# Two heads' attention scores in the two row halves of the array, with packed queries

## The chip, the cores and the metric

One Trainium2 chip, one of its cores. The metric is the device time of one execution in microseconds (us), the median of several executions. TensorE (PE) multiplies matrices into PSUM, VectorE (DVE) and ScalarE (ACT) work on SBUF and PSUM, GpSimd (POOL) on SBUF, and SyncE (SP) issues most transfers.

## What is computed

A two-layer backbone over 512 latent tokens and 256 context tokens, width 1024. Layer 0 mixes tokens with a gated delta rule, layer 1 with windowed attention, and each layer ends with an expert retrieval (PEER). The change lies in the attention of layer 1, cut here to what matters:

```python
def window_attention(q, k, v, kc, vc, sinks):     # 16 query heads, 4 key heads, head width 64
    ...
    s_loc = jnp.einsum('bnqhgd,bnkhd->bnhgqk', qb, kw).astype(F32) * scale
    ...
    s_loc = jnp.where(valid[None, :, None, None], s_loc, NEG_INF)
    s_ctx = jnp.einsum('bnqhgd,bchd->bnhgqc', qb, kc).astype(F32) * scale
    ...
    p = jax.nn.softmax(jnp.concatenate([s_loc, s_ctx, sink], axis=-1), axis=-1)
    ...
    o = (jnp.einsum('bnhgqk,bnkhd->bnqhgd', p_loc, vw)
         + jnp.einsum('bnhgqc,bchd->bnqhgd', p_ctx, vc))
```

A score sums over 64 products, half of the 128 rows of the array.

## The kernel before

The program is recorded by a framework that places buffers, sets all waits and orders the instructions of each engine by a schedule of its own. The order in which the code writes instructions is an input to that schedule and not the result. A matmul in fp32 becomes two instructions, each with its own load of 128 columns of weights.

`swa` does the attention layer in two stages. The **projection stage** (lines 776 to 845) normalizes the tokens, multiplies by six column blocks of the input weights (`columns`, tiles `pj`), rotates the result `Q` for the positions, transposes it into PSUM (`ptq`, line 830) and copies it out. One 128-row piece of `ptq` holds two heads, the first in rows 0 to 63 and the second in rows 64 to 127. Line 836 (ACT) copies the first into `qT[0:64, i]` and line 837 (DVE) the second into `qT[64:128, i + 1]`. The other 64 rows of each of the 16 query tiles are zeros, set once on POOL (line 773), and `kT` holds two key heads one above the other in the same way.

The **score stage** (lines 853 to 910) goes over four blocks of 128 queries (`b`), two pairs of key heads (`kp`) and four groups `g`: 32 pairs of heads `s` = 0, 1, so 64 heads in all. For each head:

- PE multiplies its 128-row query tile (the weights) with the 256 context keys (line 866) and with the 2 or 3 key tiles of the window (line 867), into the tile `sc`, of which there are two. Since the other head's rows of the query are zero, all 128 rows can be summed.
- PE adds the masks by a bf16 matmul with the identity (lines 871, 874): one mask in blocks 0 and 3, two in blocks 1 and 2.
- DVE takes the maximum (line 878), `mx` and `nm` (lines 879, 882); ACT the exponential `pr` (line 885), after which `sc` is free; DVE divides (`den`, lines 889 to 891).
- PE transposes `pr` into `ptp` (line 894), of which there is one; ACT or DVE copies it into `pT` (lines 896, 898).

After four pairs PE multiplies with the values (`po`, line 902), each head in one half of the array's columns. After two such rounds the block goes through the output weights (`proj`, tiles `py`). In block 0 DVE and ACT also split these weights into two parts (`wh` line 294, `wl` line 295).

Of the kernel before, what the change touches and what calls it, by code (L numbers as in the profile page):

```python
# [8 lines left out]
F32 = mybir.dt.float32  # L9
# [11 lines left out]
SEQ = 512  # L21
CTX = 256
# [42 lines left out]
class Kern:  # L65
# [697 lines left out]
    def swa(self, xl, gate, xout, done, free):  # L763

        nc, A = self.nc, self.A
        TT = CTX + SEQ
        with ExitStack() as ctx:
            q = ctx.enter_context(self.pool("sq"))
            qT = q.tile([128, 16, SEQ], F32, name="qT")
            kT = q.tile([128, 2, TT], F32, name="kT")  # L770
            vN = q.tile([128, 6, KVH, HD], F32, name="vN")
            for i in range(16):
                nc.gpsimd.memset(qT[64 - 64 * (i % 2):128 - 64 * (i % 2), i, :], 0.0)
            with ExitStack() as c1:
                ph = c1.enter_context(self.pool("sh"))
                ps = c1.enter_context(self.pool("sps", space=PSUM))
                hi = ph.tile([128, KT, TT], F32R, name="hi")
                lo = ph.tile([128, KT, TT], F32R, name="lo")

                def norm(t0, t1, row):  # L780
                    with ExitStack() as c2:
                        pn = c2.enter_context(self.pool(f"sn{row}"))
                        xs = [pn.tile([128, D], F32, name=f"x{t}") for t in range(t0, t1)]
                        for t in range(t0, t1):
                            self.dma(xs[t - t0], xl[t])
                        s = slice(t0 * 128, t1 * 128)
                        self.norm_T(1, 0, xs, [(0, t1 - t0, row)], hi[:, :, s], lo[:, :, s], pn, ps, "tp", 3)

                norm(2, 6, 0)
                p = c1.enter_context(self.pool("sp"))  # L790
                rope = p.tile([128, 4, 2, 2, 16], F32, name="rope")
                self.dma(rope, A["rope"])

                def columns(n, tiles):
                    w = [self.wsplit(p, A["s_in"][n, i], "w", [4, 256], 2, 2) for i in range(2)]
                    Q = {}
                    for t in tiles:
                        s = slice(t * 128, (t + 1) * 128)
                        pj = ps.tile([128, 256], F32, name="pj", tag="pj", bufs=3)
                        for k in range(KT):  # L800
                            wh, wl = w[k // 4]
                            self.mm3(pj, hi[:, k, s], lo[:, k, s], wh[:, k % 4, :], wl[:, k % 4, :], k == 0, k == KT - 1)
                        self.tick(TICK["swa"], MIX["swa"])
                        if n == 5:
                            nc.scalar.copy(vN[:, t].rearrange("p h d -> p (h d)"), pj)
                            continue
                        qn = Q[t] = p.tile([128, 256], F32, name="Q", tag="Q", bufs=8)
                        nc.scalar.copy(qn, pj)
                        if t < 2:
                            continue  # L810
                        x = qn.rearrange("p (h a s c) -> p h a s c", h=4, a=2, s=2)
                        rt = p.tile([128, 4, 2, 2, 16], F32, name="rt", tag="rt", bufs=2)
                        for s_ in range(2):
                            for a in range(2):
                                nc.vector.tensor_tensor(
                                    rt[:, :, a, s_, :], x[:, :, a, 1 - s_, :],
                                    rope[:, t - 2, 1, a, None, :].to_broadcast([128, 4, 16]), op=OP.mult)
                        for a in range(2):
                            nc.vector.tensor_tensor(
                                x[:, :, a], x[:, :, a],  # L820
                                rope[:, t - 2, 0, a, None, None, :].to_broadcast([128, 4, 2, 16]), op=OP.mult)
                        for s_, op in ((0, OP.subtract), (1, OP.add)):
                            nc.vector.tensor_tensor(x[:, :, :, s_, :], x[:, :, :, s_, :], rt[:, :, :, s_, :], op=op)
                    if n == 5:
                        return
                    for m in range(2):
                        for ts in (tiles[0:2], tiles[2:]) if len(tiles) == 6 else (tiles,):
                            pt = ps.tile([128, 512], F32, name="ptq", tag="tp", bufs=3)[:, 0:len(ts) * 128]
                            for i, t in enumerate(ts):
                                nc.tensor.transpose(pt[:, i * 128:(i + 1) * 128], Q[t][:, m * 128:(m + 1) * 128],  # L830
                                                    self.ident)
                            if n == 4:
                                nc.scalar.copy(kT[:, m, ts[0] * 128:(ts[-1] + 1) * 128], pt)
                            else:
                                i = 4 * n + 2 * m
                                nc.scalar.copy(qT[0:64, i, :], pt[0:64])
                                nc.vector.tensor_copy(qT[64:128, i + 1, :], pt[64:128])

                for n in range(4):
                    columns(n, range(2, 6))  # L840
                done()
                norm(0, 2, 1)
                columns(4, range(6))
                columns(5, range(6))
            free()
            with ExitStack() as c1:
                p = c1.enter_context(self.pool("sa"))
                ps = c1.enter_context(self.pool("sas", space=PSUM))
# [3 lines left out]
                for b in range(4):  # L852
                    lo_t, hi_t = max(b - 1, 0), min(b + 1, 3)
                    nl = hi_t - lo_t + 1
                    NK = CTX + nl * 128
                    tiles = [0, 1] + [2 + t for t in range(lo_t, hi_t + 1)]
                    bs = slice(b * 128, (b + 1) * 128)
                    oh = p.tile([128, KT, 128], F32R, name="oh", tag="oh", bufs=2)
                    ol = p.tile([128, KT, 128], F32R, name="ol", tag="ol", bufs=2)
                    for kp in range(2):  # L860
                        pT = [p.tile([128, 5, 4, 128], F32, name="pT", tag="pT", bufs=3) for s in range(2)]
                        for g in range(4):
                            for s in range(2):
                                i = 8 * kp + 2 * g + s
                                sc = ps.tile([128, 1024], F32, name="sc", tag="sc", bufs=2)
                                nc.tensor.matmul(sc[:, 256:512], qT[:, i, bs], kT[:, kp, 0:CTX], start=True, stop=True)
                                nc.tensor.matmul(sc[:, 512:512 + nl * 128], qT[:, i, bs],
                                                 kT[:, kp, CTX + lo_t * 128:CTX + (hi_t + 1) * 128],
                                                 start=True, stop=False, skip_group_check=True)
                                if b > 0:  # L870
                                    nc.tensor.matmul(sc[:, 512:640], self.identb, self.neg_gt, start=False,
                                                     stop=b == 3, skip_group_check=True)
# [19 lines left out]
                                pt = ps.tile([128, 8, 128], F32, name="ptp", tag="ptp", bufs=1)  # L892
# [7 lines left out]
                        for j, t in enumerate(tiles):  # L900
                            for s in range(2):
                                nc.tensor.matmul(po[64 * s:64 * s + 64, :], vN[:, t, 2 * kp + s, :],
                                                 pT[s][:, j].rearrange("p g q -> p (g q)"), start=j == 0,
                                                 stop=j == len(tiles) - 1, tile_position=(0, 64 * s),
                                                 skip_group_check=True)
# [672 lines left out]
```

## Time and profile before

| | us |
|---|---|
| median of 3 runs | 4637.15 |
| lowest and highest run | 4635.31, 4638.45 |
| the profiled execution, its own time | 4645.18 |
| span of its trace, first to last instruction | 4643.4 |
| PE busy | 3892.9 (84%) |
| DVE busy | 3152.0 (68%) |
| ACT busy | 1787.6 (38%) |
| POOL busy | 1736.7 (37%) |

The profile is one execution with every instruction's start and duration. Its times are counted from the first instruction. The projection stage lies at about 2830 to 2966 us and the score stage at 2966 to 3184. A matmul's recorded duration contains its way through the array, so the step from one matmul's start to the next one's says how long it holds the engine.

### The profile page before, as it was taken

Reading aid. Unit: us, or ns where it says so; the run is one execution under the profiler, and the core shown is the slowest. Engines: PE = TensorE matmul, PEld = TensorE weight load, DVE = VectorE, ACT = ScalarE, POOL = GpSimd, SP = SyncE. Lnnn points to the kernel's source line nnn. Section 1 sums busy time; section 2 is a strip of 40 time slices with the busy share of each in tenths; the row PEclk is TensorE's granted clock in tenths of the full one; section 3 lists DMA queues with packets and bytes.
Section 4 is the critical chain, followed back from the end, with each engine's and each line's share of the span. In section 5 each row is a group of like instructions: output and inputs, shape, how many; then the busy total and the mean of one; then the engine's idle time right before and its main releaser. Section 6 shows DMA issues by size and latency. Waiting matters only on the chain. (4 is left out here: it accounts for less than half of the span.)

```text
span 4643.4 us, 65369 instructions
## 1 busy us (share of the span) xinstructions
PE 3892.9 (84%) x23123; PEld 3128.0 (67%) x23123; DVE 3152.0 (68%) x7853; ACT 1787.6 (38%) x3426; POOL 1736.7 (37%) x1461
## 2 busy tenths in 40 slices
PE   6979999647798869999999997897946778888896
PEld 4857778545577668877877776765845666666664
DVE  3663469976699878666843445664898996767544
ACT  4764554423234733322332223443336333333332
POOL 0000011754444462565633330000340756656542
PEclk9999999878899989999999998998978899999998
DMA  6725643868888997899988883201246999999998
GB/s 234 246 93 187 213 172 100 304 241 294 284 313 279 307 379 252 336 385 368 379 324 320 320 321 131 73 19 70 90 177 189 386 353 409 409 390 409 404 393 312
DMA packets 433624, 1261.21 MB, mean 272 GB/s; under 512 B 40720, under 2 KB 139920, under 8 KB 433296
## 3 DMA queue, kind: packets, MB, share of 16 engines
q0 software_dynamic: 195680, 711.02, 40.8%
q1 hardware_dynamic: 237616, 546.01, 33.0%
q8 instruction: 182, 2.98, 0.3%
q14 instruction: 146, 1.20, 0.1%
HBM read 1177.18 MB, written 79.69 MB: 271 GB/s over the span
## 5 line engine op out<-in xcount | busy, mean ns | idle before, releaser
L1171 POOL DMA_INDIRECT u<-p_u,idx x640 | 843.7, 1318 | 723.1 <-DVE u L1173 170.4
L295 DVE TENSOR_TENSOR wl<-w,wh 128x1024 fp32r<-128x1024 f32 x604 | 735.6, 1221 | 418.0 <-ACT wh L294 408.6
L1198 POOL DMA_INDIRECT v<-p_v,idxT x640 | 719.0, 1123 | 766.0 <-PE po L1205 441.8
L294 ACT CAST wh<-w 128x1024 fp32r<-128x1024 f32 x636 | 659.8, 1046 | 887.9 <-PE pu L84 223.7
L1173 DVE SCALAR_TENSOR_TENSOR u<-u,hg 128x1024 f32<-128x1024 f32 x640 | 767.9, 1218 | 211.3 <-DMA u<-p_u,idx 209.8
L83 PE MATMUL pu<-lo,wh 128*128 128x384 f32 (+1 forms) x2048 | 658.1, 321 | 82.6 <-ACT a L1269 54.3
L85 PE MATMUL pu<-hi,wl 128*128 128x384 f32 (+1 forms) x2048 | 656.8, 321 | 52.6 <-DVE wl L295 47.9
L84 PE MATMUL pu<-hi,wh 128*128 128x384 f32 (+1 forms) x2048 | 650.6, 318 | 0.0
L83 PE MATMUL pv<-wl,ah 128*128 128x512 f32 x1280 | 527.0, 412 | 100.2 <-DVE wl L295 94.1
L84 PE MATMUL pv<-wh,ah 128*128 128x512 f32 x1280 | 512.6, 400 | 0.0
L85 PE MATMUL pv<-wh,al 128*128 128x512 f32 x1280 | 508.8, 399 | 0.0
L83 PEld LDWEIGHTS pu<-lo,wh 128*128 128x128 f32 x2048 | 406.0, 198 | 128.0 <-ACT a L1269 69.6
L85 PEld LDWEIGHTS pu<-hi,wl 128*128 128x128 f32 x2048 | 406.5, 198 | 69.9 <-DVE wl L295 59.3
L84 PEld LDWEIGHTS pu<-hi,wh 128*128 128x128 f32 x2048 | 406.2, 198 | 6.0 <-issue 5.0
L83 PEld LDWEIGHTS pv<-wl,ah 128*128 128x128 f32 x1280 | 247.0, 193 | 232.6 <-DVE wl L295 126.4
L1205 PE MATMUL po<-v,W 128*32 128x512 f32 x2560 | 322.9, 619 | 41.8 <-DMA v<-p_v,idxT 41.8
L85 PEld LDWEIGHTS pv<-wh,al 128*128 128x128 f32 x1280 | 247.8, 194 | 60.3 <-issue 5.0
L95 ACT CAST ah<-a 128x384 fp32r<-128x384 f32 (+1 forms) x256 | 116.5, 460 | 439.3 <-PE pv L84 394.5
L1269 ACT ACTIVATE a<-pu 128x384 f32<-128x384 f32 (+1 forms) x256 | 111.3, 435 | 443.2 <-PE pu L85 434.6
L84 PEld LDWEIGHTS pv<-wh,ah 128*128 128x128 f32 x1280 | 248.1, 194 | 48.9 <-issue 0.8
L295 POOL TENSOR_TENSOR wl<-w,wh 128x1024 fp32r<-128x1024 f32 x32 | 78.9, 2473 | 516.9 <-ACT wh L294 467.5
L1250 PE MATMUL pg<-oa,ob 128*128 128x128 f32 x1280 | 174.7, 291 | 56.7 <-DVE oa L1241 34.6
(483 smaller groups left out, 7114.0 us busy)
## 6 DMA issues: line engine op xcount, KB each, us to landing
w<-p_ut SPq DMA_DIRECT2D x256, 512.0 KB, 6.7
w<-p_vt SPq DMA_DIRECT2D x256, 512.0 KB, 6.8
w<-adaw SPq DMA_DIRECT2D x96, 512.0 KB, 5.2
G<-st SPq DMA_DIRECT2D x20, 2048.0 KB, 12.5
w<-g_qkv SPq DMA_DIRECT2D x48, 512.0 KB, 4.7
Gt<-G SPq DMA_DIRECT2D x32, 768.0 KB, 7.9
w<-p_wq SPq DMA_DIRECT2D x32, 512.0 KB, 4.6
Gt<-G SPq DMA_DIRECT2D x32, 512.0 KB, 7.4
```

The costliest lines, as they stand in the source:

```text
L83: mm(out, lh, rl, start=start, stop=False)
L84: mm(out, lh, rh, start=False, stop=False)
L85: mm(out, ll, rh, start=False, stop=stop)
L95: self.nc.scalar.copy(hi, x)
L294: nc.scalar.copy(hi, w)
L295: (sub or nc.vector).tensor_sub(lo, w, hi)
L1171: nc.gpsimd.indirect_dma_start(out=u, out_offset=None, in_=A["p_u"], in_offset=bass.IndirectOffsetOnAxis(ap=idx[:, s:s + 1], axis=0))
L1173: pin(nc.vector.scalar_tensor_tensor(u, u, 1.0, h, op0=OP.mult, op1=OP.mult, accum_out=w[:, s:s + 1]))
L1198: nc.gpsimd.indirect_dma_start(out=v, out_offset=None, in_=A["p_v"], in_offset=bass.IndirectOffsetOnAxis(ap=idxT[:, t:t + 1], axis=0))
L1205: pin(nc.tensor.matmul(po[hf][32 * g:32 * g + 32, :], W[:, g, :], vs[g][:, hf * 512:(hf + 1) * 512], start=j == j0, stop=j == j1 - 1, tile ...
L1250: nc.tensor.matmul(pg[:, :, j], ob[:, j, :], oa[:, j, :], start=True, stop=True)
L1269: nc.scalar.activation(a.rearrange("p g t -> p (g t)"), pu, AF.Gelu)
```

## The change

`qT` has 8 tiles of 128 rows instead of 16, each with two heads and no zeros; the memsets are gone; one ACT copy takes both heads out of `ptq`. The score matmuls take 64 rows each: head 0 in array rows 0 to 63 and head 1 in rows 64 to 127 (`tile_position`), and the code writes the matmuls of both heads alternately before the masks.

```diff
-            qT = q.tile([128, 16, SEQ], F32, name="qT")
+            qT = q.tile([128, 8, SEQ], F32, name="qT")
...
-            for i in range(16):
-                nc.gpsimd.memset(qT[64 - 64 * (i % 2):128 - 64 * (i % 2), i, :], 0.0)
...
-                                i = 4 * n + 2 * m
-                                nc.scalar.copy(qT[0:64, i, :], pt[0:64])
-                                nc.vector.tensor_copy(qT[64:128, i + 1, :], pt[64:128])
+                                nc.scalar.copy(qT[:, 2 * n + m, :], pt)
...
+                            scs = [ps.tile([128, 1024], F32, name="sc", tag="sc", bufs=2) for s in range(2)]
+                            for c0, k0, k1, last in ((256, 0, CTX, True),
+                                                     (512, CTX + lo_t * 128, CTX + (hi_t + 1) * 128, False)):
+                                for s in range(2):
+                                    r = slice(64 * s, 64 * s + 64)
+                                    nc.tensor.matmul(scs[s][:, c0:c0 + k1 - k0], qT[r, 4 * kp + g, bs], kT[r, kp, k0:k1],
+                                                     start=True, stop=last, tile_position=(64 * s, 0),
+                                                     skip_group_check=not last)
                             for s in range(2):
                                 i = 8 * kp + 2 * g + s
-                                sc = ps.tile([128, 1024], F32, name="sc", tag="sc", bufs=2)
-                                nc.tensor.matmul(sc[:, 256:512], qT[:, i, bs], kT[:, kp, 0:CTX], start=True, stop=True)
-                                nc.tensor.matmul(sc[:, 512:512 + nl * 128], qT[:, i, bs],
-                                                 kT[:, kp, CTX + lo_t * 128:CTX + (hi_t + 1) * 128],
-                                                 start=True, stop=False, skip_group_check=True)
+                                sc = scs[s]
```

What the schedule makes of it on PE, at the start of the score stage (block 0, pairs 1 and 2), before and then after. A row is a matmul with its tiles and columns, or the load of the identity for a mask; numbers tell the `sc` tiles of the heads apart in the second fence.

```order
L866 MATMUL sc<-kT,qT 128x256
L867 MATMUL sc<-kT,qT 128x256
L874 LDWEIGHTS identb
L874 MATMUL sc<-neg_lt,identb 128x128
L866 MATMUL sc<-kT,qT 128x256
L867 MATMUL sc<-kT,qT 128x256
L874 LDWEIGHTS identb
L874 MATMUL sc<-neg_lt,identb 128x128
```

```order
L864 MATMUL sc_25672<-kT_24394,qT_24393 128x256
L864 MATMUL sc_25673<-kT_24394,qT_24393 128x256
L864 MATMUL sc_25672<-kT_24394,qT_24393 128x256
L864 MATMUL sc_25673<-kT_24394,qT_24393 128x256
L874 LDWEIGHTS identb_60
L874 MATMUL sc_25672<-neg_lt_64,identb_60 128x128
L874 LDWEIGHTS identb_60
L874 MATMUL sc_25673<-neg_lt_64,identb_60 128x128
L864 MATMUL sc_25718<-kT_24394,qT_24393 128x256 x2
L874 LDWEIGHTS identb_60
L874 MATMUL sc_25718<-neg_lt_64,identb_60 128x128
L864 MATMUL sc_25719<-kT_24394,qT_24393 128x256 x2
```

In pair 1 the two heads' matmuls stand alternately. From pair 2 on, both matmuls of head 0 stand together, then its mask, then both of head 1; so it is in all of the other 31 pairs, here the first of block 1 on PE after the change:

```order
L864 MATMUL sc_26231<-kT_24394,qT_24393 128x256
L864 MATMUL sc_26231<-kT_24394,qT_24393 128x384
L871 LDWEIGHTS identb_60
L871 MATMUL sc_26231<-neg_gt_62,identb_60 128x128
L874 LDWEIGHTS identb_60
L874 MATMUL sc_26231<-neg_lt_64,identb_60 128x128
L864 MATMUL sc_26232<-kT_24394,qT_24393 128x256
L864 MATMUL sc_26232<-kT_24394,qT_24393 128x384
L871 LDWEIGHTS identb_60
L871 MATMUL sc_26232<-neg_gt_62,identb_60 128x128
```

In blocks 1 to 3 the rows of PE, DVE and ACT stand as they did before, but for the line number of the scores. In block 0 DVE's order has moved, here after its first two maxima, before and then after the change:

```order
L889 TENSOR_TENSOR den<-sm 128x1
L878 TENSOR_REDUCE mx<-sc 128x1
L890 RECIPROCAL den<-den 128x1
L879 TENSOR_SCALAR mx<-mx,sink 128x1
L891 TENSOR_SCALAR pr<-pr,den 128x512
L878 TENSOR_REDUCE mx<-sc 128x1
L882 TENSOR_SCALAR nm<-mx 128x1
L295 TENSOR_TENSOR wl<-w,wh 128x1024
```

```order
L889 TENSOR_TENSOR den<-sm 128x1
L890 RECIPROCAL den<-den 128x1
L891 TENSOR_SCALAR pr<-pr,den 128x512
L295 TENSOR_TENSOR wl<-w,wh 128x1024
L878 TENSOR_REDUCE mx<-sc 128x1
L295 TENSOR_TENSOR wl<-w,wh 128x1024
L879 TENSOR_SCALAR mx<-mx,sink 128x1
L878 TENSOR_REDUCE mx<-sc 128x1
```

The first maximum of pair 2 now stands behind the division of pair 1 and one weight split, and a second split stands between the two maxima.

## Rows read from the trace of the kernel before

**Rows 1.** Windows: projection stage and blocks 0 to 3; busy us per engine, granted clock.

```profile
core 0: us, PE busy (x) PEld busy (x) DVE busy (x) ACT busy (x) POOL busy (x), PEclk, DMA share, GB/s
2872.00:2966.00 94.00, 91.19 (x730) 88.90 (x729) 49.57 (x187) 32.49 (x65) 0.00 (x0) 0.98 0.18 57
2966.00:3016.00 50.00, 34.40 (x154) 22.48 (x153) 36.33 (x106) 27.31 (x61) 0.00 (x0) 0.90 0.34 116
3016.00:3072.00 56.00, 52.20 (x306) 35.94 (x306) 38.89 (x114) 23.03 (x60) 0.00 (x0) 1.00 0.06 20
3072.00:3129.00 57.00, 53.12 (x313) 36.44 (x312) 39.23 (x114) 23.05 (x59) 0.00 (x0) 1.00 0.06 19
3129.00:3184.00 55.00, 46.90 (x285) 34.08 (x284) 38.32 (x121) 22.28 (x65) 0.00 (x0) 1.00 0.03 10
```

**Rows 2.** Timeline of PE, one pair in block 1 (start, us, instruction).

```profile
3067.11 0.70 PE L866 MATMUL sc<-kT,qT 128*128 128x256 f32 x2
...
3068.35 0.22 PE L874 MATMUL sc<-neg_lt,identb 128*128 128x128 bf16 x1
3068.40 0.65 PE L866 MATMUL sc<-kT,qT 128*128 128x256 f32 x2
...
3069.59 0.22 PE L874 MATMUL sc<-neg_lt,identb 128*128 128x128 bf16 x1
...
3072.22 0.70 PE L866 MATMUL sc<-kT,qT 128*128 128x256 f32 x2 [0.21 <-ACT pr L885]
```

**Rows 3.** Timeline of DVE and ACT in the same pair.

```profile
3069.85 0.82 DVE L878 TENSOR_REDUCE mx<-sc 128x1 f32<-128x640 f32 x1
...
3071.05 0.14 DVE L882 TENSOR_SCALAR nm<-mx 128x1 f32<-128x1 f32 x1
...
3071.29 0.79 ACT L885 ACTIVATE pr<-sc,nm 128x640 f32<-128x640 f32 x1 [0.19 <-DVE nm L882]
```

**Rows 4.** Views of the tiles qT and ptq and of line 773, whole program.

```profile
L866 PE MATMUL sc<-kT,qT x128: 377/382/764, 2966.1 to 3179.4; 128*128 128x256 f32 x128
L773 POOL MEMSET qT<- x16: 517/520/524, 2799.1 to 2807.7; 64x512 f32 x16
L836 ACT COPY qT<-ptq x8: 577/579/581, 2891.7 to 2931.8; 64x512 f32<-64x512 f32 x8
L837 DVE COPY qT<-ptq x8: 686/690/695, 2892.3 to 2932.6; 64x512 f32<-64x512 f32 x8
...
  PE pt L268: 0.4, 1
```

**Rows 5.** Timeline of PE where matmuls in column halves (L902) begin and end.

```profile
3020.65 1.07 PE L902 MATMUL po<-pT,vN 128*64 128x512 f32 x2
3021.66 0.38 PE L83 MATMUL py<-wl,oh 128*128 128x256 f32 x1
3021.88 0.28 PE L84 MATMUL py<-wh,oh 128*128 128x256 f32 x1
3022.00 0.28 PE L85 MATMUL py<-wh,ol 128*128 128x256 f32 x1
...
3024.32 0.22 PE L874 MATMUL sc<-neg_lt,identb 128*128 128x128 bf16 x1
3024.47 3.65 PE L902 MATMUL po<-pT,vN 128*64 128x512 f32 x14
```

**Rows 6.** Timeline of PE in layer 0, matmuls of 32 columns (L85) and 32 rows (L332).

```profile
262.35 0.40 PE L85 MATMUL pa<-lhi,awl 128*32 128x512 f32 x1
262.58 1.02 PE L537 MATMUL pe<-rr,cm 128*128 128x512 f32 x2
263.44 0.38 PE L538 MATMUL pe<-neg_lt,identb 128*128 128x512 bf16 x1
263.75 0.43 PE L332 MATMUL pa<-cm,abT 32*128 32x32 f32 x4
```

**Rows 7.** Timeline of PE and DVE, a pair of block 3.

```profile
3176.73 0.22 PE L871 MATMUL sc<-neg_gt,identb 128*128 128x128 bf16 x1
...
3177.26 0.68 DVE L878 TENSOR_REDUCE mx<-sc 128x1 f32<-128x512 f32 x1
```

## The prediction

> **What bounds the kernel now.** I read first the windows of the two stages that the change touches [rows 1]. In the projection stage PE is busy 91.2 of 94 us, so PE bounds it. In the score stage PE is idle 15.6 of 50 us in block 0, 3.8 of 56 in block 1, 3.9 of 57 in block 2 and 8.1 of 55 in block 3, while DVE, the next, is busy 36 to 39 us in each. So blocks 1 and 2 are close to PE's limit, while in blocks 0 and 3 waits between the engines count too. Then the timeline of one pair in block 1, to see which chain closes the circle. The scores of head 0 start at 3067.11 and the next pair's at 3072.22, a period of 5.11 us [rows 2]. Within it the scores and masks of both heads run without a pause until 3069.81 (the last mask's 3069.59 and its 0.22) [rows 2]; the maximum of head 1 follows at once, at 3069.85, and DVE's next rows up to `nm` at 3071.05 stand behind it in DVE's order; the exponential at 3071.29 waits for `nm` [rows 3]; when it is done, at 3072.08, `sc` is free and the next scores start 0.14 us later [rows 2, 3]. The score matmuls of both heads lie on this circle. What makes one of them longer makes the pair longer by as much.
>
> **The change, part by part.** The sum is made for the profiled execution (4645.18 us by its own time, span 4643.4), which took 8.0 us longer than the median of the runs, 4637.15; the 8.0 are taken off at the end.
>
> *Memsets.* 16 of 0.52 us on POOL, 8.3 us, go [rows 4]. They ran at 2799 to 2808, and the first reader of the query tiles starts at 2966.1 [rows 4]; that distance hides them. POOL has nothing else in either stage [rows 1]. Worth nothing; without that cover it would be 8.3 us.
>
> *Copies.* Eight DVE copies of 0.69 us go; the eight ACT copies of 0.58 us keep their 512 columns and take 128 rows instead of 64 [rows 4]. No row shows that rows cost time, and DVE has 44 us to spare in that stage [rows 1]. PE waited for the DVE copy once, 0.4 us [rows 4]. Between 0 and 0.4 us gained; I take 0.4.
>
> *The matmuls themselves.* Their number, their columns and the columns of weights stay. The gain would be that two heads run side by side. Matmuls in two column halves do that: 14 of them, each of 512 columns, take 3.65 us [rows 5]. An fp32 column takes about 0.85 ns here (from 3068.40 to 3069.59 stand 2 × 256 and 2 × 384 columns and one mask of 0.05 [rows 2], and two passes at 2.4 GHz are 0.83), so 512 take 0.43, and one after another the 14 would take 6.0 us. But that needs both heads' matmuls next to each other in PE's order, and the order shows this in pair 1 alone. In the other 31 pairs the masks of head 0, which take all 128 rows, stand between them: the `sc` tile of head 0 becomes free before that of head 1, and the schedule fills it at once. So of 32 pairs one gains, some 0.9 us of streaming, just before PE waits for the first exponentials anyway. I count nothing.
>
> *Going in and out of the halves.* Before, scores, masks and transposes all took the whole array. Whatever follows a mask starts 0.05 us after it, the time of its 128 bf16 columns (3068.35 to 3068.40) [rows 2]. Where the column halves begin, the step from the mask is 0.15 (3024.32 to 3024.47), 0.10 more [rows 5]. Where they end, two matmuls of 0.43 and the first load, 0.05, would bring 3020.65 to 3021.56; the next matmul starts at 3021.66, 0.10 more, and the one behind it 0.22 later instead of 0.12, since the first one's weights were not loaded ahead: another 0.10 [rows 5]. The only matmuls with fewer rows in this program, 32 rows in layer 0, start 0.31 after a matmul of 512 bf16 columns (0.21 at 2.4 GHz): again 0.10 more [rows 6]. So for each head I count 0.10 to enter, 0.10 for the first load of query weights, 0.10 to leave, and 0.03 to 0.10 for the first load of the mask's identity: 0.33 to 0.40, and I take 0.34. The lower end of the unknown is 0, since the row halves themselves are in no row of before, and one kind of narrow matmul pays nothing (second rival). The Trainium skill says in TensorEngine Tiling (Array Packing), Key Properties, that changing the tiling mode, not just the tile, drains TensorE. By that sentence each of the 31 pairs without neighbours drains four times; it gives no price, so the price stays that of the rows.
>
> *What of it lies on the path.* Blocks 1 and 2 have 16 pairs. Both heads are on the circle there, and PE has too little idle time to hide them: 32 × 0.34 = 10.9 us. In block 3, 8 pairs: the mask of a pair's second head ends at 3176.95 and its maximum starts at 3177.26 because DVE was busy [rows 7], so 0.31 of its 0.34 are covered; the first head has no such cover. 8 × 0.34 + 8 × 0.03 = 3.0; with no cover it would be 5.4. In block 0, 7 pairs pay; PE waits most there, and I let one head in two count: 7 × 0.34 = 2.4, between 0 and 4.8. DVE's new order there puts weight splits of 1.2 us before other maxima than it did; three of them more or fewer on the path are 3.6 us either way, and I take 0. Outside, the order of some 60 rows moves (a few transposes in the projections, some rows of layer 1's experts); nothing in them is added, and I give them 2 us either way.
>
> *Behind the stage.* The first weights of layer 1's routing now wait for ACT too, but stand on SP's queue behind loads of the attention's result, which come later. So what the score stage loses reaches the end.
>
> Sum: −0.4 + 10.9 + 3.0 + 2.4 = +15.9 us. 4645.2 + 15.9 = 4661.1 for a profiled execution, less 8.0 is **4653 us** for the median, 0.34% slower. About 0.2% (9.3 us) is what a measurement of this kernel can tell from no change, so the bounds are 4628 and 4646.
>
> **The rivals.**
>
> *Price paid, but hidden by waits.* PE's idle time in the stage is 15.6 + 3.8 + 3.9 + 8.1 = 31.4 us [rows 1], more than the whole price of 63 × 0.34 = 21.4. If DVE and ACT reach their limits first wherever they now nearly do, half of the sum stays: +8, 4645 us. Against it stand blocks 1 and 2, where the circle contains the matmuls.
>
> *No price.* The 32-column matmuls of layer 0 that use one place of the array alone are followed after 0.23 us for 512 columns [rows 6], as in any run of such matmuls. If a 64-row tile followed by a full mask is like this case, nothing changes but the 0.4: 4637 us. Against it stand the 32-row matmuls, whose start does show the 0.10.
>
> *The halves do run side by side: faster.* If PE's order, or PE itself past the order, let the two heads overlap in all pairs, a pair would stream one head's columns instead of two: 1.07 us less in blocks 1 and 2 (256 and 384 columns, four passes at 2.4 GHz) and 0.85 in the others, and would go in and out once. On the shares taken above that is −17 − 7 for the streams and +9 for the price of 32 excursions: −15, 4622 us. It decides wherever a mask no longer stands between two heads. For it speaks that column halves overlap in this very trace; against it the order, in which 31 of 32 pairs are split. The Trainium skill's page TensorEngine Tiling (Array Packing), Theoretical Speedup, gives up to 2 times for 64 rows; by it the score matmuls would take half, which is this rival and needs the neighbours as well.
>
> *A higher price.* If within a half the weights of the second key range are not loaded ahead either, each head pays two or three more loads of 0.10, and the lower pace lets the clock fall more often than the 0.90 that block 0 shows [rows 1]: +30, 4667 us.
>
> **How the numbers follow.** Chances: my forecast 0.50, hidden by waits 0.15, no price 0.20, side by side 0.05, higher price 0.10. The forecast's own range is 4646 to 4660, from 0.33 to 0.40 a head and the bounds of blocks 0 and 3. The range for 8 in 10 must take in no price and hidden by waits, and leaves out side by side and most of the higher price: 4634 to 4663. Slower by over 0.2%: nearly all of the forecast (0.49), the higher price and a third of the hidden case, 0.64. Within 0.2%: 0.31. Faster: 0.05.
>
> **What would show it.** After the change, in pairs of block 1: the step from the last score matmul to the first mask 0.1 longer than the columns, the loads of a score's first weights no longer ahead of the matmul, and the mask after them likewise; a period near 5.8 us instead of 5.11 where the exponential closes the circle; block 3 longer by 3 us, blocks 1 and 2 by 5 to 6 each. In pair 1 two score matmuls of different heads starting within 0.05 us of each other. The memsets' end and the copies should show as no shift of the first score matmul by more than 1 us. I am wrong if the masks follow the scores without a gap, or if DVE, not PE, ends the waits in blocks 1 and 2, or if the new order of block 0 alone moves its length by more than 4 us.

## The result, and the profile after

The changed kernel took 4671.7 us in the median of 4 runs (4654.5 to 4677.8), the kernel before 4637.8 beside it: a ratio of 1.0075, with a 95% interval of 1.0053 to 1.0096, so some 34 us slower. Beside the first experiments it was timed again: 4661.2 us in 6 runs, 1.0054 (1.0036 to 1.0073). Over these runs the mean is 4664.5 us for the changed kernel (10 runs) and 4636.9 for the kernel before (the 73 runs beside the experiments): 28 us more. The two measurements side by side give 34 and 22, so the 28 is itself known to some 6 us only. The forecast was 16 more, 4653 us, with a range up to 4663.

The profiled execution of the changed kernel took 4654.5 us, 10 less than the mean of its kernel, while that of the kernel before took 8 more than its own. So whole spans can't be compared, and the stage is read by itself. The windows of PE, cut at the first score matmul of each block and at the first transpose of layer 1's norm behind the last projection (us and length, busy time and instructions, granted clock, DMA share, GB/s), of the changed kernel:

```profile
core 0: us, PE busy (x), PEclk, DMA share, GB/s
2957.74:3011.04 53.30, 43.35 (x154) 0.71 0.32 109
3011.04:3074.19 63.15, 59.62 (x307) 0.92 0.05 18
3074.19:3134.22 60.03, 56.39 (x312) 1.00 0.05 18
3134.22:3227.42 93.20, 74.40 (x399) 0.87 0.10 36
```

and the last of these four windows in the kernel before; its first three are those of [rows 1] to within 0.3 us (50.19, 55.97 and 57.17 us, at 0.90, 1.00 and 1.00):

```profile
3129.39:3214.44 85.05, 65.52 (x399) 0.94 0.12 42
```

The reader is to see two things. Block 2 has the full clock in both and is 2.9 us longer. Blocks 0, 1 and 3 are 3.1, 7.2 and 8.2 us longer, and their clock is lower: 0.71, 0.92 and 0.87 instead of 0.90, 1.00 and 0.94. Twice the missing share times the length is the time at 1.2 GHz: 31 us of block 0 instead of 10, 10 us of block 1 instead of none, 24 instead of 10 in the last window. The four windows are 21.3 us longer together.

The last window needs care. In three further profiles of the changed kernel (table and samples below) it takes 89.2 to 89.8 us at 0.94, the clock of the kernel before, and most of the 10 us at 1.2 GHz that such a window shows lies at its end, where PE is idle for some 10 us ahead of the norm's transpose. The changed kernel, profiled again:

```profile
3141.76:3230.99 89.23, 69.64 (x399) 0.94 0.10 38
```

So the lower clock of the last window is the reading of one profile in four.

PE's timeline of the last pair of block 1, the one that answers to [rows 2] (start, us, instruction; in brackets the idle time before it and what ended it):

```profile
3068.72 1.34 PE L864 MATMUL sc<-kT,qT 64*128 64x256 f32 x4
3070.00 0.23 PE L871 MATMUL sc<-neg_gt,identb 128*128 128x128 bf16 x1
3070.06 0.22 PE L874 MATMUL sc<-neg_lt,identb 128*128 128x128 bf16 x1
3070.21 1.34 PE L864 MATMUL sc<-kT,qT 64*128 64x256 f32 x4
3071.49 0.23 PE L871 MATMUL sc<-neg_gt,identb 128*128 128x128 bf16 x1
3071.55 0.22 PE L874 MATMUL sc<-neg_lt,identb 128*128 128x128 bf16 x1
3071.61 0.72 PE L894 MATMUL ptp<-cm,pr 128*128 128x128 f32 x5
...
3074.19 0.48 PE L864 MATMUL sc<-kT,qT 64*128 64x256 f32 x1 [0.21 <-ACT pr L885]
```

From the second mask of head 0 to the scores of head 1 it is now 0.15 us, in [rows 2] 0.05: entering costs 0.10, as forecast. From the first score to the transposes it is 2.89 us, in [rows 2] 2.53 (3067.11 to 0.05 behind 3069.59), and the period grows from 5.11 to 5.47 us. So a pair pays 0.36, not the 0.68 of the forecast, and eight pairs of such a block 2.9.

Pair 1, the only one in which the two heads' matmuls alternate, in the same timeline:

```profile
2957.74 1.66 PE L864 MATMUL sc<-kT,qT 64*128 64x256 f32 x8
2959.34 0.29 PE L874 MATMUL sc<-neg_lt,identb 128*128 128x128 bf16 x2
```

Its eight matmuls of 256 columns take 1.60 us to the mask, hardly less than the 1.7 that eight of 256 columns at 0.85 ns would take one after another, though going in and out is in the 1.60 too. By the single starts, two matmuls of the one head begin 7 ns after one of the other (2958.276 and 2958.283, 2958.596 and 2958.603); the other four run one after another.

Where the clock is lost PE is not idle. Two windows of the changed kernel in block 0:

```profile
2970.00:2980.00 10.00, 9.37 (x26) 0.50 0.53 177
2980.00:2990.00 10.00, 8.55 (x25) 0.50 0.31 107
```

PE is busy 9.37 and 8.55 of 10 us and stays at 1.2 GHz, where the kernel before has 0.90 over the block with a busy share of 0.69 [rows 1]. In both kernels the clock first falls at the end of the wait of over 4 us behind pair 1; in the kernel before it then has 0.62 to 0.80 from 2970.06 to 2982.06, in steps of 4 us, and 1.00 from 2986.06 to 2998.06, in the changed kernel 0.50 all the way from 2965.74 to 2993.74.

### The profile page after: what moved, and what is told of

The parts are those of the page before. It is cut to its first block, busy times and chain, and to the rows that moved or that the text cites. A ratio compares the mean times of both kernels' runs of the same rounds, so it can differ in the third digit from the quotient of the medians.

```text
span 4652.7 us, 65323 instructions
## 1 busy us (share of the span) xinstructions
PE 3916.3 (84%) x23123; PEld 3124.8 (67%) x23123; DVE 3152.0 (68%) x7845; ACT 1789.0 (38%) x3426; POOL 1740.0 (37%) x1445
## 5 line engine op out<-in xcount | busy, mean ns | idle before, releaser
L1198 POOL DMA_INDIRECT v<-p_v,idxT x640 | 728.4, 1138 | 752.7 <-PE po L1205 427.1
L85 PE MATMUL pu<-hi,wl 128*128 128x384 f32 (+1 forms) x2048 | 653.4, 319 | 48.9 <-DVE wl L295 43.7
L85 PE MATMUL pv<-wh,al 128*128 128x512 f32 x1280 | 508.9, 399 | 0.0
L85 PEld LDWEIGHTS pu<-hi,wl 128*128 128x128 f32 x2048 | 402.6, 197 | 67.0 <-DVE wl L295 55.6
L85 PEld LDWEIGHTS pv<-wh,al 128*128 128x128 f32 x1280 | 246.3, 192 | 59.1 <-issue 4.2
```

Source lines behind the costliest of these rows:

```text
L85: mm(out, ll, rh, start=False, stop=stop)
L1198: nc.gpsimd.indirect_dma_start(out=v, out_offset=None, in_=A["p_v"], in_offset=bass.IndirectOffsetOnAxis(ap=idxT[:, t:t + 1], axis=0))
```

## The experiments

Three theories. A: only the going in and out of the halves costs. B: the halves also let TensorE's clock fall. C: the new order of block 0 on DVE and ACT costs the rest. Median and ratio of each kernel (beside runs of the kernel before on the same chip; the interval is 95%), and from its profile the length of the four windows in us, with the granted clock:

| kernel | us | ratio | block 0 | block 1 | block 2 | block 3 and projection |
|---|---|---|---|---|---|---|
| before | 4632 to 4639 | 1 | 50.2 (0.90) | 56.0 (1.00) | 57.2 (1.00) | 85.1 (0.94) |
| changed, again | 4661.2 | 1.0054 (1.0036 to 1.0073) | 53.2 (0.68) | 63.1 (0.92) | 60.0 (1.00) | 89.2 (0.94) |
| e1_halves | 4679.1 | 1.0092 (1.0078 to 1.0107) | 55.5 (0.69) | 63.2 (0.92) | 60.0 (1.00) | 96.8 (0.82) |
| e2_order | 4639.1 | 0.9996 (0.9986 to 1.0006) | 51.1 (0.87) | 56.0 (1.00) | 57.2 (1.00) | 86.1 (0.93) |
| e3_switch | 4652.0 | 1.0023 (1.0012 to 1.0034) | 50.6 (0.83) | 59.4 (1.00) | 60.3 (1.00) | 87.3 (0.95) |
| e4_mid | 4644.1 | 1.0026 (1.0014 to 1.0038) | 50.4 (0.90) | 58.8 (1.00) | 60.0 (1.00) | 85.0 (0.95) |
| e5_ends | 4656.4 | 1.0053 (1.0036 to 1.0070) | 55.6 (0.69) | 56.1 (1.00) | 57.2 (1.00) | 96.5 (0.82) |
| e6_adjacent | 4881.5 | 1.0532 (1.0507 to 1.0556) | 121.7 (0.66) | 124.5 (0.63) | 122.9 (0.67) | 121.4 (0.64) |
| e7_pinfull | 4912.5 | 1.0596 (1.0573 to 1.0618) | 128.6 (0.68) | 131.4 (0.70) | 133.1 (0.69) | 126.9 (0.70) |
| e8_onetile | 4703.8 | 1.0162 (1.0141 to 1.0184) | 70.2 (0.68) | 75.7 (0.82) | 76.3 (0.81) | 99.9 (0.81) |
| e9_onefull | 4739.1 | 1.0221 (1.0201 to 1.0241) | 75.1 (0.72) | 83.7 (0.83) | 85.4 (0.82) | 105.2 (0.84) |
| e10_fill | 4663.8 | 1.0068 (1.0055 to 1.0082) | 56.4 (0.70) | 59.7 (1.00) | 60.0 (1.00) | 92.3 (0.97) |
| e11_fullfill | 4645.8 | 1.0024 (1.0012 to 1.0035) | 49.9 (0.93) | 57.0 (1.00) | 57.2 (1.00) | 89.0 (0.96) |
| e12_fill16 | 4673.7 | 1.0072 (1.0049 to 1.0095) | 53.4 (0.90) | 72.9 (0.88) | 60.0 (1.00) | 99.7 (0.97) |
| e13_fullfill16 | 4657.4 | 1.0041 (1.0026 to 1.0056) | 50.8 (0.93) | 61.7 (1.00) | 57.2 (1.00) | 96.2 (0.96) |

**The parts of the change, each alone.** e1_halves takes the kernel before and gives only the two score matmuls 64 rows:

```diff
-nc.tensor.matmul(sc[:, 256:512], qT[:, i, bs], kT[:, kp, 0:CTX], start=True, stop=True)
+r, tp = slice(64 * s, 64 * s + 64), (64 * s, 0)
+nc.tensor.matmul(sc[:, 256:512], qT[r, i, bs], kT[r, kp, 0:CTX], start=True, stop=True, tile_position=tp)
...
```

> The row halves alone: the kernel before with its memsets, its 16 query tiles, its copies and its order of code, only the two score matmuls of a head read 64 rows at (0,0) or (64,0). PE's order in the score stage stays that of the kernel before but for a few transposes of block 0. Theory A (going in and out of the halves is all that costs): +14 to +17 us over the kernel before, granted clock in block 0 as before, about 0.90. Theory B (half of the rows lets TensorE's clock fall as well): +28 to +40 us, and block 0's granted clock near 0.67 as in the changed kernel. Theory C (the changed order of block 0 on DVE and ACT costs the rest): as A here, since that order is not taken over.

e2_order writes the score matmuls of both heads alternately, as the change does, and leaves them on 128 rows:

```diff
+scs = [ps.tile([128, 1024], F32, name="sc", tag="sc", bufs=2) for s in range(2)]
...
+for s in range(2):
+    nc.tensor.matmul(scs[s][:, c0:c0 + k1 - k0], qT[:, 8 * kp + 2 * g + s, bs],
+                     kT[:, kp, k0:k1], start=True, stop=last, skip_group_check=not last)
```

> The order of code alone: score matmuls of both heads written alternately as in the changed kernel, but over all 128 rows with the zeros, memsets and copies of the kernel before. Theories A and B: within 4 us of the kernel before. Theory C: +10 us or more.

e3_switch puts a 64-row matmul of two columns ahead of each head's full-array scores:

```diff
+nc.tensor.matmul(sc[:, 0:2], qT[r, i, bs], kT[r, kp, 0:2], start=True, stop=True, tile_position=(64 * s, 0))
 nc.tensor.matmul(sc[:, 256:512], qT[:, i, bs], kT[:, kp, 0:CTX], start=True, stop=True)
```

> The going in and out alone, with the array full while columns stream: the kernel before with one more matmul of 2 columns on 64 rows ahead of each head's scores (it writes columns of the score tile that nobody reads). It pays 0.3 us a head for going in and out, and some 0.1 to 0.3 for its own load and passes: 64 heads, of which about 50 count, +15 to +30 us, the same under all theories in time. What tells them apart is the clock: Theory A and C: what e1_halves loses is lost here too. Theory B: block 0's granted clock stays near 0.90, since the score matmuls use all rows, while in e1_halves it falls.

The changed kernel itself ran beside them:

> The changed kernel again, beside the three others on one chip: +30 to +36 us over the kernel before under all theories. Theory B: a profile that took longer than the one shown (span 4652.7) has more half clock in the score stage, above all in block 0 and the last block; theories A and C: the same clock and the difference elsewhere.

The changed kernel lost 22 us here in the medians, not the 30 to 36 expected. The halves alone cost more than the whole change, 40 us in the medians, and the code's order costs nothing. That speaks against C but does not rule it out: the schedule orders the rows of DVE and ACT in block 0 anew in e1_halves and in e2_order too, in each in a way of its own, so neither has the changed kernel's order. What rules it out for the clock are the pairs of equal order below. In block 0 the changed kernel is 2.3 us shorter than e1_halves (53.2 and 55.5). e3_switch goes in and out for every head as well, for one more matmul of two columns, but its scores stream over all rows: blocks 1 and 2 grow by 3.4 and 3.1, block 0 by 0.4, and the total by some 11 us, less than the 15 to 30 expected. What e1_halves loses beyond that goes with its clock: 0.69, 0.92 and 0.82 against 0.83, 1.00 and 0.95. But 0.83 is also below the 0.90 that theory B expected here (0.89 to 0.93 in three profiles of the kernel before), so going in and out may lower the clock of block 0 by itself; its one profile, in an order of its own on every engine, doesn't settle that.

**Where it is lost.** e4_mid and e5_ends are e1_halves with the condition `b in (1, 2)` or `b in (0, 3)` on the rows; e4_mid has the order of the kernel before on every engine, e5_ends that of e1_halves.

> Row halves in blocks 1 and 2 alone (32 of the 64 heads), everything else, the order on every engine too, as in the kernel before. Going in and out on the path costs 2.8 us a block at full clock (block 2 of the changed kernel and of e1_halves: 60.0 us against 57.2). Theory B (the clock falls where 64-row matmuls meet a stage in which PE has waits): blocks 0 and 3 keep the clock of the kernel before, block 1 starts from a raised clock and keeps it, so +5 to +8 us. Theory A (only the going in and out costs, each excursion alike): half of what e1_halves lost, +20 us.

> Row halves in blocks 0 and 3 alone, the order on every engine as in e1_halves. Theory B: +25 to +35 us, nearly all that e1_halves lost, with some 34 us of half clock in block 0 again and the clock still low when block 1 begins. Theory A: +20 us, and less if PE's waits in these blocks hide it.

Blocks 0 and 1 of e1_halves, block 1 of e4_mid and block 1 of e5_ends:

```profile
2965.44:3020.97 55.53, 44.77 (x153) 0.69 0.31 105
3020.97:3084.12 63.15, 59.61 (x306) 0.92 0.05 17
...
3010.73:3069.56 58.83, 55.31 (x306) 1.00 0.06 19
...
3030.33:3086.47 56.14, 52.16 (x307) 1.00 0.05 20
```

In the middle blocks alone the halves cost 2.9 us a block at full clock and nothing elsewhere. Block 1, which has 7.2 us more in the changed kernel, has 2.9 here: its other 4.3 us come with its low clock. That clock isn't left over from block 0. In the changed kernel, where block 1 begins at 3011.04, it is back at 1.00 some 14 us earlier and falls anew (all engines, then the granted clock):

```profile
2997.00:3007.00 10.00, 9.12 (x46) 4.86 (x45) 6.11 (x20) 5.34 (x15) 0.00 (x0) 1.00 0.00 0
3007.00:3017.00 10.00, 8.51 (x32) 4.44 (x30) 6.91 (x24) 2.63 (x9) 0.00 (x0) 0.74 0.00 0
3017.00:3027.00 10.00, 9.53 (x37) 5.02 (x38) 3.82 (x13) 3.42 (x10) 0.00 (x0) 0.75 0.01 2
```

It is at 1.00 up to 3011.04 and at 0.50 from 3013.04. With halves in block 0 alone (e5_ends) block 1 keeps 1.00, though a low clock at its start was expected, and so it does with halves in block 1 alone (e4_mid): this fall needs halves on both sides of the border. In the first and last block alone they cost 5.4 and 11.5 us at a clock of 0.69 and 0.82. Theory A, with the same price for each excursion, does not give this. The totals fit B less well than the windows do: e4_mid lost 12 us in the medians, more than the 5 to 8 of B (A said 20), of which its windows show 5.8; e5_ends lost 25, the low end of 25 to 35, of which its windows show 17.

**Is it the clock?** e10_fill adds to e1_halves, and e11_fullfill to the kernel before, eight matmuls a head whose result nobody reads, in blocks 0 and 3; e12_fill16 and e13_fullfill16 add sixteen. In each of the two sets the order on every engine is the same, so that its kernels differ by the row halves alone.

```diff
+for j in range(8 if b in (0, 3) else 0):
+    nc.tensor.matmul(pt[:, 7, :], self.identb, self.neg_gt, start=True, stop=True)
 for j in range(NK // 128):
     nc.tensor.transpose(pt[:, j, :], pr[:, j * 128:(j + 1) * 128], self.ident)
```

> The kernel e1_halves (row halves, order of code of the kernel before) with work that does nothing: in blocks 0 and 3 eight more full-array matmuls of 128 bf16 columns ahead of each head's transposes, into columns of their tile that nobody reads. At full clock they are 0.43 us a head, half of what the score streams lost in busy rows there. Theory B1 (half-busy rows let the clock fall): block 0's half clock comes down from 34 us to 20 or less, and block 0 is no longer than in e1_halves (55.5) although PE has 7 us more to do. Theory A or C (not the clock): half clock stays near 34 us and block 0 gets longer by up to 7 us.

> The control of e10_fill: the same filling matmuls in the kernel before, with the same order on every engine as e10_fill, so that these two differ by the row halves alone. Theory B1: e10_fill less this one is smaller than e1_halves less the kernel before (40 us): +10 to +25. Theory A or C: the same 40 us. If the 10 us of half clock that the kernel before has in block 0 are gone here, this one may be up to 5 us faster than the kernel before, else up to 14 us slower.

> e10_fill with sixteen filling matmuls a head in blocks 0 and 3 instead of eight. If the clock alone is what is left in block 0: the half clock there falls from 34 us to 15 or less, and block 0 gets shorter than e10_fill's 56.4 us although PE has 7 us more work at full clock; it is then 2 to 4 us longer than in e13_fullfill16. If something else holds block 0 back, its half clock stays near 34 us and it gets longer than 60 us, or the clock comes back and the block does not get shorter.

> The control: sixteen filling matmuls a head in the kernel before, with the same order on every engine as e12_fill16. Block 0 49 to 55 us with less than 10 us of half clock; e12_fill16 less this one is +10 to +14 us for the whole program if only going in and out is left (2.8 us a block), more if the clock still falls in one of them.

Windows of PE, block 0 and ten us of it, of e10_fill

```profile
2963.84:3020.27 56.43, 51.04 (x254) 0.70 0.31 103
...
2970.00:2980.00 10.00, 10.00 (x40) 0.50 0.46 166
```

and of e11_fullfill

```profile
2960.00:3009.85 49.85, 37.68 (x255) 0.93 0.34 117
...
2970.00:2980.00 10.00, 6.38 (x50) 1.00 0.43 135
```

With the halves PE is busy without a pause and stays at 1.2 GHz; with all rows it is busy 6.38 of 10 us and has 2.4 GHz. In blocks 1 and 3 the filling was enough: the clock is that of the control, and what is left is 2.7 and 3.3 us (59.7 and 57.0, 92.3 and 89.0). In the medians e10_fill is 18 us longer than e11_fullfill, within the 10 to 25 that theory B1 gave, where e1_halves had lost 40. In block 0 eight were not enough: it has 34 us at 1.2 GHz, as e1_halves has, against B1's forecast of 20 or less, and is 6.6 us longer than its control. Sixteen were. Block 0 of e12_fill16

```profile
2959.15:3012.58 53.43, 46.04 (x337) 0.90 0.31 109
```

and of e13_fullfill16

```profile
2965.24:3016.07 50.83, 41.40 (x338) 0.93 0.34 115
```

With twice the filling block 0 is shorter than in e10_fill, by 3.0 us, and 2.6 us longer than its control: the price of going in and out, and no more. In block 3 that price is 3.5 (99.7 and 96.2, at 0.97 and 0.96). Elsewhere e12_fill16 missed: block 1 is 11.2 us longer than in the control and fell to 0.88, and the totals are 16 us apart instead of the 10 to 14 expected, so the two kernels together are no proof of a total.

**Would the halves pay if they were neighbours?** e6_adjacent fixes the order of the scores and masks of a pair in the changed kernel (`self.pin(...)` around each of these matmuls keeps them in the order of the code), e7_pinfull is the same with full-array matmuls. e8_onetile gives a pair one score tile of four banks, so that both heads become free at once, and writes both heads' masks behind the four score matmuls; e9_onefull is its control with all rows and zeros.

```diff
-scs = [ps.tile([128, 1024], F32, name="sc", tag="sc", bufs=2) for s in range(2)]
+sc2 = ps.tile([128, 2, 1024], F32, name="sc", tag="sc", bufs=1)
+scs = [sc2[:, s] for s in range(2)]
```

> The changed kernel with the scores and masks of a pair kept in the order of the code, so that in all 32 pairs the matmuls of both halves are neighbours in PE's order and run side by side. It saves 0.85 to 1.07 us of streaming in each pair and goes in and out once instead of twice (0.17 a head on the path): 16 pairs of blocks 1 and 2 give 16 x (1.07 - 0.35) = 11.5 us back against the kernel before, less what head 0 loses by waiting for both score tiles. Theory B1 (the chip counts the rows that are busy): with both halves busy the clock in blocks 0 and 3 is as in the kernel before, total -20 to 0 us. Theory B2 (the chip counts the time that PE is busy, or the halves as such): the halves make PE idle longer and the clock falls as in the changed kernel or more, total +10 to +30 us.

> The control of e6_adjacent: the same fixed order of scores and masks with full-array matmuls and zeros. What it loses against the kernel before is the price of the fixed order (head 0 waits for both score tiles): 0 to +15 us under all theories; e6_adjacent minus this is the effect of the halves side by side.

> The changed kernel with one score tile of four banks for a pair (one buffer) instead of a tile of two banks for each head (two buffers), and the masks of both heads written behind all four score matmuls. Both halves then become free at the same time, and in PE's order the score matmuls of both heads are neighbours in all 32 pairs, with the transposes of the pair before behind them. In blocks 1 and 2 a pair streams 1.07 us less and goes in and out once, not twice: 16 x (1.07 - 0.17) = 14 us less than the kernel before, if nothing is lost by waiting for both heads' exponentials; with the clock of the changed kernel in blocks 0 and 3 (+16 us) the sum is near 0 for Theory B2 (idle time of PE lowers the clock), and -10 to -20 us for Theory B1 (busy rows count, and both halves are busy). If the wait for the whole tile ends the pairs, +10 to +40 us, and e9_onefull shows it too.

> The control of e8_onetile: the same single score tile and nearly the same order on PE, with full-array matmuls and zeros. Against the kernel before it shows what the single tile costs (0 to +40 us); e8_onetile less this one is what the halves side by side give: -20 to -30 us for all theories by the streams, since e6_adjacent was 31 us faster than e7_pinfull.

All four lost, and far more than expected: e6_adjacent 250 us in the medians (−20 to +30), e7_pinfull 281 (0 to 15), e8_onetile 66 (at most 40), e9_onefull 101 (0 to 40). The heads of a pair now wait for each other: in the fixed order the transposes of head 0 stand ahead of the masks of head 1, and with one tile PE waits 41 us of blocks 1 and 2 for the division (`pr`, DVE) ahead of a transpose. But each with halves beat its control, by 31 and 35 us in the medians. PE's timeline of a pair of block 2, at 2.4 GHz, in e8_onetile

```profile
3158.60 1.35 PE L865 MATMUL sc<-kT,qT 64*128 64x256 f32 x8
3159.88 0.23 PE L871 MATMUL sc<-neg_gt,identb 128*128 128x128 bf16 x1
```

and of one in e9_onefull, at 2.4 GHz too

```profile
3157.12 2.32 PE L868 MATMUL sc<-kT,qT 128*128 128x256 f32 x8
3159.28 0.22 PE L874 MATMUL sc<-neg_gt,identb 128*128 128x128 bf16 x1
```

The eight matmuls of a pair take 1.28 us in halves and 2.16 over the whole array. The Trainium skill gives up to 2 times for 64 rows (TensorEngine Tiling (Array Packing), Theoretical Speedup); with going out included the trace shows 1.7. In both kernels the clock is near 0.8 in the middle blocks, where PE now has long waits, so this says nothing on the clock of filled halves.

**Samples.** Two more profiles of each kernel:

> The changed kernel, one more profile: block 0 with 30 to 34 us of half clock, block 1 with 10, block 2 with none. If it takes 4665 us or more and the score stage explains that, its last block and the projection behind it have more than the 24.5 us of half clock of the first profile, or block 1 has more than 10; else the loss lies outside the score stage.

> The changed kernel, another sample of the same: block 0 with 30 to 34 us of half clock, block 1 with 10, block 2 with none, and the same reading of the last block if it takes 4665 us or more.

> The kernel before, one more profile. If the stage explains the whole loss, its four blocks take 238 to 241 us instead of 248.4, with no half clock in block 0; if not, they take 247 to 250 again, and the time ahead of the stage and behind it is 4380 to 4390 us, less than the mean of 4393 in the four profiles of the changed kernel.

> The kernel before, another sample of the same: blocks of 238 to 241 us in sum if the stage explains the whole loss, 247 to 250 us and less time around the stage if it does not.

The changed kernel took 4668.4 and 4666.1 us there, with windows of 53.2, 63.1, 60.0, 89.7 and 53.1, 63.2, 60.0, 89.8. The kernel before took 4651.9 and 4654.8, with 48.3, 56.0, 57.2, 83.5 and 48.2, 56.0, 57.2, 84.8. Over four and three profiles the stage is 266.8 and 246.5 us: 20.3 us longer, and never more than 25. So the stage explains some 20 of the 28 us, and these profiles do not show the others. In the changed kernel the last window has 11 us at 1.2 GHz, not the more than 24.5 that was to explain so long a run. In the kernel before the four blocks take 245 and 246 us, which is neither of the two sums expected. And the rest of the span was 4383 to 4401 us in the changed kernel and 4395 to 4407 in the kernel before, 9.5 us less in the mean and not more.

## Why the prediction was wrong

The sign and the place were right: the scores' stage got longer, by going in and out of the halves. The size was forecast as 16 us, and about 28 came (34 in the first measurement). That blocks 1 and 2 together lost 10.0 us, close to the 10.9 forecast, is luck: 5.7 of it is the price of the halves, 4.3 the clock in block 1.

*The memsets, the copies, the stage behind.* The first score matmul started at 2957.7 to 2969.6 us in four profiles of the changed kernel and at 2966.1 to 2977.5 in three of the kernel before; against that spread the 0.4 us cannot be seen. What the stage lost was not seen to come back behind it: 1424 to 1438 us follow in the changed kernel, 1429 to 1432 in the kernel before.

*The matmuls themselves.* As read from the order: 31 pairs split, one side by side in part. The Trainium skill's sentence that changing the tiling mode drains TensorE (TensorEngine Tiling (Array Packing), Key Properties) agrees with the 0.10 us each way of the trace.

*Going in and out* was counted too high. The 0.10 to enter and the 0.10 to leave are there. But head 0 of a pair enters while PE waits for its tile anyway, and its first load was not ahead of its matmul before either; head 1's first load cost 0.05, since before it was not fully hidden (0.65 and 0.70 us for two matmuls in [rows 2] show the difference); and the identity's load cost 0.01. So a pair in blocks 1 and 2 pays 0.36 instead of 0.68, and the two blocks 5.7 us instead of 10.9 (e4_mid). Blocks 0 and 3 came out as forecast, if the pairs with filling are taken for the price: 2.6 us for 2.4 (e12_fill16 less e13_fullfill16), 3.3 to 3.5 for 3.0. Going in and out is 11.7 us in all, for 16.3. The way out is read against the first mask of either head in the kernel before, in the pair of [rows 2]:

```profile
3068.29 0.22 PE L871 MATMUL sc<-neg_gt,identb 128*128 128x128 bf16 x1
...
3069.53 0.22 PE L871 MATMUL sc<-neg_gt,identb 128*128 128x128 bf16 x1
```

From a head's first score to it there are 1.18 and 1.13 us (3067.11 and 3068.40), after the change 1.28 for both heads.

*The clock* is the step that failed. The sum held no term for it; the fall stood only in the rival of a higher price, at 0.10, beside loads within a half that would not be ahead (they are: those 1.28 us are 0.10 and 0.15 more than before, the way out and, for head 1, its first load). With the price alone the stage loses 11.7 us; it lost 20.3. The other 8.6 lie in block 0 (4.3 over the means of the profiles, less 2.6), block 1 (7.2 less 2.9) and the last window (6.0 less 3.4). Block 1's 4.3 go with a clock that fell in all four profiles and in none of e4_mid and e5_ends. Block 0's 1.7 are the clock's loss and whatever its new order gives or takes. Of the last window's 2.6 only 0.9 go with the clock, which fell in one profile of four; the other three are still 5.1 us longer than the kernel before, and what the 1.7 beyond the price are is not shown. So the clock took at least 5 us of the stage, and more if the new order of block 0 gained something. That the halves cause the fall in block 0 is shown by e10_fill and e11_fullfill, which differ in nothing else: 0.70 and 0.93, and 6.6 us. Whether fewer busy rows do it or the going in and out that comes with them is not separated, since e3_switch has 0.83 there with scores over all rows.

*The new order of block 0* was given 0, between −3.6 and +3.6. No run measures it: the 2.3 us between the changed kernel and e1_halves stand between two new orders, and e2_order, with a third one, is 0.9 us longer in block 0 than the first profile of the kernel before.

*What stays open.* Some 8 us of the 28, as e1_halves, e4_mid and e5_ends too lost 6 to 13 us more in the medians than in their windows. The mean granted clocks of the timed runs give 728 us at 1.2 GHz for the changed kernel and 669 for the kernel before, 59 more, of which the profiles find 38 in the stage; the others may carry the 8 us, but no profile shows where. Open are also the 1.7 us of the last window, why the clock there falls more often in e1_halves than in the changed kernel (0.82 and mostly 0.94), and how the chip weighs a half-used array.

## What to carry to other kernels

Two halves of the array can pay only where their matmuls are neighbours in PE's order (and even there no kernel here came below the kernel before): read that order first, since a scheduler fills the tile that becomes free first, and one full-array instruction in between turns the gain into a price of 0.10 us each way. Count that price only on the side of an instruction that does not wait anyway. And where a stage has waits and its clock already dips, ask what the halves do to the clock, and read the granted clock of each stretch: a PE that is busy 94% of the time can be a PE at 1.2 GHz.

## What was not expected of the hardware

Score matmuls on 64 rows went with a clock of 0.69 in a block that has 0.90 on 128 rows, with more busy time of PE, not less: 44.8 of 55.5 us in e1_halves, 34.4 of 50 in [rows 1]. Part of that busy time is the low clock itself: the eight matmuls of a pair in e8_onetile take 2.44 us to the mask at 1.2 GHz and 1.28 at 2.4. But the busy time did not bring the clock back. Full-array matmuls between them brought it back, eight a head in block 3 and sixteen in block 0. The Trainium skill says that the clock is set by how busy PE has been (TensorE: Matmul & The Clock Gate, Part 1); ten us of e10_fill with PE busy throughout at 1.2 GHz do not agree with that, if busy means time.
